# A two-instruction exchange on ScalarE and a reordered close of the last down projection in a one-layer encoder kernel

## The chip, the cores and the metric

The kernel runs as one program on one core of a Trainium2 chip. The metric is the device time of one execution in microseconds, given as the median of several runs. The five engines of the core are called PE (TensorE, matrix products), ACT (ScalarE), DVE (VectorE), POOL (GpSimd) and SP (SyncE, which here only issues DMAs).

## The reference, cut to what matters

One layer of a streaming encoder: two mixers, a cross attention to a memory, and an MLP, each added to the residual stream `h` (512 frames of width 1024), and a final RMSNorm. All is float32. The change lies in the MLP and in the final norm:

```python
def rmsnorm(x, g):
    y = xf * lax.rsqrt(jnp.mean(xf * xf, axis=-1, keepdims=True) + EPS)
    return y * g
...
u = rmsnorm(h, norm_ff_g) @ w1            # (512, 1024) @ (1024, 4096)
h = h + jnp.square(jax.nn.relu(u)) @ w2   # (512, 4096) @ (4096, 1024)
return rmsnorm(h, final_norm_g)           # (512, 1024)
```

## The kernel before

**Precision.** Each float32 operand of a product is split into a high and a low part (`hi` = a rounded copy, made by ACT; `lo` = operand - `hi`, made by DVE at L183, L1549/L1551 or L1580/L1582), and a product is three matmuls: hi x hi, hi x lo, lo x hi.

**The MLP.** The 4096 hidden units are eight groups of 512 (`g` = 0 to 7). Each group's up projection and down projection is a 2 x 2 block product done with seven block products instead of eight, named "1" to "7"; their operands are blocks or sums of blocks (`comb`, `wsum`, `block_sum`). `PRODUCTS` is the order in which PE takes them; the very first group has an order of its own, `FIRST` ("1", "2", "5", "6", "7", "3", "4"). For group 0 the parts of weights and activations are made in an order written out by hand (the `manual_schedule` block at L1798 to L1839); there `split_first("6", "h")` is the ACT copy `whu06` of a summed weight block for product 6, and `x_hi_of("5", slice(0, 2))` is the ACT copy of the first half of the activation sums for product 5 (tile `xs_hi`).

**The last pair.** Groups 0 to 5 are projected down one at a time. Groups 6 and 7 are projected down together at the end (`mlp_down((6, 7))`): for each product in the order 1, 5, 6, 2, 7, 3, 4, PE runs group 6 and then group 7, each for two 128-row halves `t` = 0, 1. A weight block is `wrd` when loaded, `whd` and `wld` when split; the hidden operand's two parts are `hb`. Names carry group and product: `whd63` belongs to group 6, product 3. Products accumulate in PSUM banks `U` (products 1, 6, 7, 4), `Y` (5, 3) and `V` (2), and DVE adds or subtracts a finished bank to `acc` (`add_to`, L1595 and L1597). `acc` has four tiles of 128 frames x 1024: product 3 ends with `acc0` and `acc1`, products 7 and 4 end with `acc2` and `acc3`.

**The close.** `finish` is called when a half row of an `acc` tile is final. For the first half of a tile, ACT takes the sum of squares (`fj`, `fe`), POOL multiplies the half by the norm's weight (`fa`). For the second half of `acc0` and `acc1` it only notes the work in `deferred`. Product 4 is written out in `last_product` (L1659 to L1712) with ACT and DVE in program order: PE takes the rows of `acc2` into bank `U` (to which `onto_rows` had added `acc2`), and those of `acc3` in two column halves, `Z0` and `Z1`. In its shadow ACT and DVE square the rest of `acc0` and `acc1`, POOL raises the sums to the power -1/2 (`fr`, L1720), ACT scales the half with `fa` (`scale_a`, L1728), DVE the other (`scale_b`, L1737), and SP issues the output: tiles 0 and 1 whole (512 KB each), tile 2 in two halves, tile 3 in two halves, one of them from ACT's queue.

**What sets the order.** PE runs in program order throughout. Outside the blocks marked `manual_schedule` a list scheduler orders ACT, DVE, POOL and SP by priority, so moving two instructions can shift others later. Buffers come from rotating pools (four `wh`, four `wl`, twelve of 4 KB per partition tagged `s4`).

Of the kernel before, what the change touches and what calls it, by code (L numbers as in the profile page):

```python
# [13 lines left out]
ALU = mybir.AluOpType  # L14
# [32 lines left out]
def emit(  # L47
# [49 lines left out]
    def s4(shape, name, dt=F32):  # L97
        return s4p.tile([P] + shape, dt, tag="s4", name=name)
# [18 lines left out]
    def mm(name, shape=(S,)):  # L117
        return mmp.tile([P] + list(shape), F32, tag="mm", name=name)
# [10 lines left out]
    def f(a):  # L129
        return a.bitcast(F32)  # L130
# [1433 lines left out]
    hb_order += [(g, name) for name in PRODUCTS for g in (NG - 2, NG - 1)]  # L1564
    hb_used = [0]

    def behind_w4(at, n):
        order_only = mybir.DependencyInfo(mybir.DependencyClass.NoSync, mybir.DependencyReason.DATA)
# [2 lines left out]
    def hidden_part(g, name):  # L1571

        src = comb[g][name]
        hb = s4([2, 2, HS], f"hb{g}{name}", R)
        sign = -1.0 if name == "6" else 1.0
        at = ac.activation(hb[:, 0], src, AF.Copy, scale=sign)
        if g == 0 and name == "1":
            behind_w4(at, 0)
        if name == "6":
            ve.scalar_tensor_tensor(hb[:, 1], src, -1.0, f(hb[:, 0]), op0=ALU.mult, op1=ALU.subtract)  # L1580
        else:
            ve.tensor_tensor(hb[:, 1], src, f(hb[:, 0]), ALU.subtract)  # L1582
        hbs[g, name] = hb

    def hidden_ahead(key, n, within=None):
# [6 lines left out]
    def add_to(ps, rows, half, t, sign):  # L1592
        a = acc[2 * rows + t][:, half * S : (half + 1) * S]
        if sign > 0:
            ve.tensor_tensor(a, ps, a, ALU.add)  # L1595
        else:
            ve.scalar_tensor_tensor(a, ps, -1.0, a, op0=ALU.mult, op1=ALU.add)  # L1597

    PLAN = {
        "1": ("U", True, ()),  # L1600
# [8 lines left out]
    def mlp_down(gs):  # L1609

        end = gs[-1] == NG - 1
        banks = {}
        for n, name in enumerate(PRODUCTS):
            bank, first_, goes = PLAN[name]
            if end and name == PRODUCTS[-1]:
                last_product(gs, banks)
                return
            for g, t in [(g, t) for g in gs for t in range(2)]:
                whi, wlo = unit("d", g, name)
                hidden_ahead((g, name), 1)  # L1620
                hb = hbs[g, name]
                if first_ and g == gs[0]:
                    banks[bank, t] = {"U": sc, "Y": tr}[bank](f"{bank}{g}{t}")
                ps = banks[bank, t]
                ts_ = slice(t * P, (t + 1) * P)
                for k in range(2):
                    hi, lo = hb[:, 0, k, ts_], hb[:, 1, k, ts_]
                    begin = first_ and g == gs[0] and k == 0
                    te.matmul(ps, hi, whi[:, k, :], start=begin, stop=False, skip_group_check=True)  # L1629
                    te.matmul(ps, hi, wlo[:, k, :], start=False, stop=False, skip_group_check=True)  # L1630
                    at = te.matmul(ps, lo, whi[:, k, :], start=False, stop=k == 1, skip_group_check=True)  # L1631
                presum.tick(6 * S / 2400, at)
                if end and (g, t) == (gs[0], 1):
# [12 lines left out]
            hidden_ahead((gs[-1], name), HB, gs)  # L1646
            yield

    onto = []

    def onto_rows(banks):

        u0, u1, a = banks["U", 0], banks["U", 1], acc[3]
        ve.tensor_tensor(u0, u0, acc[2][:, 0:S], ALU.add)
        onto.append(mm("Z1")[:, 0:HS])
        ve.tensor_tensor(onto[0], u1[:, HS:S], a[:, HS:S], ALU.add)
        ve.tensor_tensor(a[:, 0:HS], u1[:, 0:HS], a[:, 0:HS], ALU.add)

    def last_product(gs, banks):  # L1659

        name = PRODUCTS[-1]

        def steps(g, t, cols):
            (whi, wlo), hb = unit("d", g, name), hbs[g, name]
            for k in range(2):
                hi, lo = (hb[:, x, k, t * P : (t + 1) * P] for x in range(2))
                yield from ((hi, whi[:, k, cols]), (hi, wlo[:, k, cols]), (lo, whi[:, k, cols]))

        def product(ps, t, cols, start):
            ops = [op for g in gs for op in steps(g, t, cols)]  # L1670
            for i, (a, b) in enumerate(ops):
                te.matmul(ps, a, b, start=start and i == 0, stop=i == len(ops) - 1, skip_group_check=True)

        with tc.manual_schedule(engines={mybir.EngineType.Activation, mybir.EngineType.DVE}):
            u0 = banks["U", 0]
            product(u0, 0, slice(0, S), False)
            o2, o3 = s4([D], "fo2"), s4([D], "fo3")
            (half, o0, r0_), (_, o1, r1_) = deferred
            hs = slice(half * S, (half + 1) * S)
            e0 = sm(1, "fv0")  # L1680
            ac.activation(o0[:, hs], acc[0][:, hs], AF.Square, scale=1.0 / 32.0, accum_out=e0)
            gp.tensor_tensor(e0, e0, fin[0][0], op=ALU.add)
            row_scale(r0_, e0)
            row_scale(r1_, squares(acc[1][:, hs], o1[:, hs], fin[1][0], "fv1"))
            e2, e3, r2_, r3_ = sm(1, "fv2"), sm(1, "fv3"), sm(1, "fr2"), sm(1, "fr3")
            scale_b(0, half, o0, r0_)
            ac.activation(o2[:, 0:S], u0, AF.Square, scale=1.0 / 32.0, accum_out=e2)
            gp.tensor_tensor(e2, e2, fin[2][0], op=ALU.add)
            row_scale(r2_, e2)
            scale_a(0, o0, r0_)  # L1690
            scale_a(1, o1, r1_)
            scale_b(1, half, o1, r1_)
            for tb, o in ((0, o0), (1, o1)):
                nc.sync.dma_start(out[rows_(tb), :], o)
            h0, h1 = slice(0, HS), slice(HS, S)
            z0, z1 = mm("Z0")[:, 0:HS], onto[0]
            product(z0, 1, h0, True)
            ve.tensor_tensor(acc[3][:, h0], z0, acc[3][:, h0], ALU.add)
            v3 = squares(acc[3][:, h0], o3[:, h0], fin[3][0], "fv30")
            scale_b(2, 0, o2, r2_, u0)  # L1700
            nc.sync.dma_start(out[rows_(2), 0:S], o2[:, 0:S])
            product(z1, 1, h1, False)
            ac.activation(o3[:, h1], z1, AF.Square, scale=1.0 / 32.0, accum_out=e3)
            scale_a(2, o2, r2_)
            dma_a(nc.sync, 2, o2)
            ve.tensor_tensor(e3, e3, v3, ALU.add)
            row_scale(r3_, e3)
            scale_a(3, o3, r3_)
            dma_a(ac, 3, o3)
            for cs, src in ((h0, acc[3][:, h0]), (h1, z1)):  # L1710
                ve.scalar_tensor_tensor(o3[:, cs], src, r3_, gfin[0][:, cs], op0=ALU.mult, op1=ALU.mult)
            nc.sync.dma_start(out[rows_(3), 0:S], o3[:, 0:S])  # L1712

    def squares(a, o, v0, name):
        v = sm(1, name)
# [3 lines left out]
    def row_scale(r, v):  # L1719
        gp.tensor_tensor(r, v, mhalf[:, 0:1], op=ALU.pow)  # L1720
        return r
# [12 lines left out]
    def scale_b(tb, half, o, r, src=None):  # L1734
        cs = slice(half * S, (half + 1) * S)
        src = acc[tb][:, cs] if src is None else src
        ve.scalar_tensor_tensor(o[:, cs], src, r, gfin[half], op0=ALU.mult, op1=ALU.mult)  # L1737


    FINAL = (("2", 0), ("7", 1), ("3", 0))  # L1740
# [2 lines left out]
    def finish(tb, half):  # L1743
# [3 lines left out]
        if tb not in fin:  # L1747
# [4 lines left out]
            gp.tensor_tensor(ag, a[:, cs], gfin[half], op=ALU.mult)  # L1752
# [152 lines left out]
```

## Time and profile before

| what | us |
|---|---|
| median of 3 runs (lowest, highest) | 753.86 (753.45, 754.28) |
| the profiled execution | 753.76 |
| its span, first to last instruction | 751.8 |
| busy in the span: PE | 743.0 (99%) |
| busy in the span: DVE / ACT / POOL | 544.6 / 440.7 / 202.3 |

The span is what the views measure; about 2 us of the execution's own time lie outside it. PE's granted clock was 0.998 of full speed. The last matmul starts at 745.21, so 6.5 us of the span come after it. A timeline row gives start, duration, engine, source line, operation, output <- inputs, shapes and count, and in brackets how long the engine stood idle before it and what ended that. A window row gives for each engine its busy time and instruction count, then PE's clock, the DMA engines' mean busy share and GB/s.

### The profile page before, as it was taken

The page shows a single profiled execution, that of the slowest core. Times are in us where ns is not written, and L with a number is a line of the kernel's source. Part 1 is how long each engine was busy: PE and PEld are TensorE (multiplying, and loading weights), DVE is VectorE, ACT ScalarE, POOL GpSimd, SP SyncE. Part 2 cuts the span into 40 slices and gives each one's busy share as a digit, 9 for nine tenths or more (in the row PEclk, how much of TensorE's full clock was granted, in tenths as well). Part 3 has the DMA queues.
Part 4 walks back from the last instruction along what each step waited for, and adds up shares of the span by engine and source line. Part 5 has one row for each costly group of instructions (what it writes and reads, how often), then busy time and mean ns, then how long its engine had stood idle before and what let it go on. Part 6 is the DMA issues. An engine that isn't in the chain of part 4 may idle for free.

```text
span 751.8 us, 12385 instructions
## 1 busy us (share of the span) xinstructions
PE 743.0 (99%) x4645; PEld 652.7 (87%) x4645; DVE 544.6 (72%) x859; ACT 440.7 (59%) x735; POOL 202.3 (27%) x279
## 2 busy tenths in 40 slices
PE   9999999999999999999999999999999999999996
PEld 6889888888888988888888899898989899999985
DVE  5647873677878756645555799978787887878796
ACT  5655555655666532334434589766566757574863
POOL 7207531233433227621111212111111111100034
PEclk9999999999999999999999999999999999999999
DMA  8641987567957789986578799998989898977452
GB/s 249 200 116 58 307 263 224 182 223 258 294 183 224 261 223 210 196 165 123 121 168 191 118 246 230 245 218 243 239 219 233 221 252 212 243 190 231 134 112 112
DMA packets 109677, 152.92 MB, mean 203 GB/s; under 512 B 6145, under 2 KB 75818, under 8 KB 109618
## 3 DMA queue, kind: packets, MB, share of 16 engines
q1 hardware_dynamic: 85458, 112.52, 45.9%
q0 software_dynamic: 24000, 39.35, 30.3%
q8 instruction: 36, 0.59, 0.3%
q10 hardware_dynamic: 160, 0.27, 0.1%
q14 instruction: 23, 0.19, 0.1%
HBM read 147.91 MB, written 51.40 MB: 265 GB/s over the span
## 4 chain that ended last, share of the span: by engine, by line
PE 91%; DVE 4%; ACT 2%; issue 1%; POOL 1%; DMA 1%; POOLq 0%; SPq 0%; DVEq 0%; ACTq 0%
PE uU L1474 4%; PE uU L1475 4%; PE uU L1473 4%; PE U L1629 3%; PE U L1630 3%; PE U L1631 3%; PE xq L253 2%; PE wo L253 2%; PE xq L254 2%; PE xq L255 2%; PE xw L253 2%; PE xw L254 2%; PE wo L255 2%; PE wo L254 2%; PE uY L1475 2%; PE uY L1474 2%
## 5 line engine op out<-in xcount | busy, mean ns | idle before, releaser
L183 DVE TENSOR_TENSOR wlu<-wru,whu 128x1024 fp32r<-128x1024 f32 x53 | 64.0, 1226 | 26.3 <-ACT whu L179 26.2
L179 ACT ACTIVATE whu<-wru 128x1024 fp32r<-128x1024 f32 x53 | 55.7, 1058 | 41.2 <-PE U L1631 16.8
L183 DVE TENSOR_TENSOR wld<-wrd,whd 128x1024 fp32r<-128x1024 f32 x56 | 69.1, 1236 | 13.8 <-ACT whd L179 13.6
L179 ACT ACTIVATE whd<-wrd 128x1024 fp32r<-128x1024 f32 x56 | 59.0, 1053 | 14.0 <-PE uU L1474 6.3
L1629 PE MATMUL U<-whd,hb 128*128 128x512 f32 x120 | 46.8, 390 | 0.0
L1630 PE MATMUL U<-wld,hb 128*128 128x512 f32 x120 | 46.8, 390 | 0.0
L1631 PE MATMUL U<-whd,hb 128*128 128x512 f32 x120 | 46.7, 389 | 0.0
L1014 POOL TENSOR_SCALAR bi<-nF,Ft 128x128 f32<-128x128 f32 (+3 forms) x32 | 20.8, 656 | 60.4 <-PE pt L1046 33.8
L1474 PE MATMUL uU<-xs_lo,whu 128*128 128x256 f32 x128 | 36.3, 284 | 0.2 <-DVE xs_lo L1549 0.2
L1473 PE MATMUL uU<-xs_hi,whu 128*128 128x256 f32 x128 | 36.3, 284 | 0.0
L1475 PE MATMUL uU<-x_hi,wlu 128*128 128x256 f32 x128 | 36.2, 283 | 0.0
L1473 PE MATMUL uY<-xs_hi,whu 128*128 128x256 f32 x128 | 36.2, 283 | 0.0
L1474 PE MATMUL uY<-xs_lo,whu 128*128 128x256 f32 x128 | 36.2, 283 | 0.0
L1475 PE MATMUL uY<-xs_hi,wlu 128*128 128x256 f32 x128 | 36.2, 283 | 0.0
L1474 PE MATMUL uU<-x_lo,whu 128*128 128x256 f32 x128 | 36.2, 283 | 0.0
L1475 PE MATMUL uU<-xs_hi,wlu 128*128 128x256 f32 x128 | 36.2, 283 | 0.0
L1473 PE MATMUL uU<-x_hi,whu 128*128 128x256 f32 x128 | 36.2, 283 | 0.0
L444 POOL DMA_DIRECT2D wsd<-in_w_dram x16 | 17.8, 1116 | 63.7 <-PE xw L255 12.8
L1369 POOL DMA_DIRECT2D wrd<-in_w_dram x8 | 9.8, 1220 | 86.9 <-DVE wld L183 76.4
L444 POOL DMA_DIRECT2D wsu<-in_w_dram x14 | 17.1, 1220 | 48.2 <-PE xw L255 15.6
L1631 PEld LDWEIGHTS U<-whd,hb 128*128 128x128 f32 x120 | 22.5, 188 | 4.8
L1629 PEld LDWEIGHTS U<-whd,hb 128*128 128x128 f32 x120 | 22.6, 188 | 4.5
(958 smaller groups left out, 2621.2 us busy)
## 6 DMA issues: line engine op xcount, KB each, us to landing
wru<-in_w_dram SPq DMA_DIRECT2D x25, 512.0 KB, 8.0
wsd<-in_w_dram SPq DMA_DIRECT2D x24, 512.0 KB, 7.0
wrd<-in_w_dram SPq DMA_DIRECT2D x24, 512.0 KB, 4.4
wrd<-wsd SPq DMA_DIRECT2D x24, 512.0 KB, 6.0
wsu<-in_w_dram SPq DMA_DIRECT2D x21, 512.0 KB, 6.8
wru<-wsu SPq DMA_DIRECT2D x21, 512.0 KB, 5.8
wsd<-in_w_dram POOLq DMA_DIRECT2D x16, 512.0 KB, 6.6
wsu<-in_w_dram POOLq DMA_DIRECT2D x14, 512.0 KB, 7.1
```

The lines of the kernel that those rows point to most:

```text
L179: at = ac.activation(hi, raw, AF.Copy)
L183: at_lo = ve.tensor_tensor(lo, raw, f(hi), ALU.subtract)
L253: te.matmul(ps, wh, hi, start=n_ == 0 and not begun, stop=False)
L254: te.matmul(ps, wh, lo, start=False, stop=False)
L255: at = te.matmul(ps, wl, hi, start=False, stop=k == order[-1])
L444: yield gp.dma_start(wsum[kind, g, name], src, accum_op=ALU.add, **more)
L1473: te.matmul(ps[:, i, :], whi[:, k, ws], xh[:, k, :], start=begin, stop=False, skip_group_check=True)
L1474: te.matmul(ps[:, i, :], whi[:, k, ws], xl[:, k, :], start=False, stop=False, skip_group_check=True)
L1475: at = te.matmul(ps[:, i, :], wlo[:, k, ws], xh[:, k, :], start=False, stop=k == UK - 1, skip_group_check=True)
L1629: te.matmul(ps, hi, whi[:, k, :], start=begin, stop=False, skip_group_check=True)
L1630: te.matmul(ps, hi, wlo[:, k, :], start=False, stop=False, skip_group_check=True)
L1631: at = te.matmul(ps, lo, whi[:, k, :], start=False, stop=k == 1, skip_group_check=True)
```

## The change

There are three edits. The first exchanges two neighbouring ACT instructions in the hand-written start of the MLP. On ACT, before:

```order
L179 ACTIVATE whu05_4556<-wr05_4504 128x1024
L1538 ACTIVATE xs_hi_4594<-xd5_4562 128x512
L179 ACTIVATE whu06_4601<-wr06_4506 128x1024
L1508 ACTIVATE xg7_4605<-hT3_3287,gv_239 128x512
L1805 ACTIVATE x2_hi_4146<-hT3_3287,gv_239 128x512
L1538 ACTIVATE xs_hi_4594<-xd5_4562 128x512
```

And with the change, on ACT at the same place:

```order
L179 ACTIVATE whu05_4556<-wr05_4504 128x1024
L179 ACTIVATE whu06_4600<-wr06_4506 128x1024
L1539 ACTIVATE xs_hi_4594<-xd5_4562 128x512
L1509 ACTIVATE xg7_4605<-hT3_3287,gv_239 128x512
L1799 ACTIVATE x2_hi_4146<-hT3_3287,gv_239 128x512
L1539 ACTIVATE xs_hi_4594<-xd5_4562 128x512
```

The weight copy for product 6 now stands ahead of the first activation copy for product 5; the rows around them stay. (Line numbers behind the edits differ by a few.) The scheduler also swaps a handful of neighbours in the second group, where the sums of squares of `acc0` and `acc1` (`sj`) now stand ahead of the split of `wru12`.

The second edit changes the order of the last pair's products to 1, 5, 6, 2, 3, 7, 4, takes product 7 by row half first (both groups for `t` = 0, then both for `t` = 1), and does the second half of `finish` for tiles 0 and 1 at once. The third has tile 2 leave as one DMA and tile 3 as one 256 KB half from ACT and two 128 KB quarters from SP. Two order-only dependencies pin DVE: the last low half, `hb74`, ahead of the subtraction that makes `acc2`, and the addition of `acc2` into bank `U` ahead of the two output scalings. On DVE, over the last products, before:

```order
L1582 TENSOR_TENSOR hb73_7776<-s3_7_7562,hb73_7776 128x512
L1582 TENSOR_TENSOR hb64_7779<-sq61_6922,hb64_7779 128x512
L183 TENSOR_TENSOR wld73_7761<-wrd73_7670,whd73_7760 128x1024
L1582 TENSOR_TENSOR hb74_7832<-sq71_7325,hb74_7832 128x512
L183 TENSOR_TENSOR wld64_7783<-wrd66_7465,whd64_7782 128x1024
L1597 SCALAR_TENSOR_TENSOR acc2_4315<-U60_7579,acc2_4315 128x512
L1597 SCALAR_TENSOR_TENSOR acc3_4316<-U61_7586,acc3_4316 128x512
L1654 TENSOR_TENSOR U60_7579<-U60_7579,acc2_4315 128x512
L1656 TENSOR_TENSOR Z1_7813<-U61_7586,acc3_4316 128x256
L1657 TENSOR_TENSOR acc3_4316<-U61_7586,acc3_4316 128x256
L183 TENSOR_TENSOR wld74_7817<-wrd76_7498,whd74_7816 128x1024
L1597 SCALAR_TENSOR_TENSOR acc0_4313<-Y60_7626,acc0_4313 128x512
```

And with the change, on DVE at the same place (`fo0`, `fo1` are the output rows of tiles 0 and 1):

```order
L1585 TENSOR_TENSOR hb64_7779<-sq61_6922,hb64_7779 128x512
L183 TENSOR_TENSOR wld77_7761<-wrd77_7670,whd77_7760 128x1024
L183 TENSOR_TENSOR wld64_7783<-wrd66_7465,whd64_7782 128x1024
L1599 SCALAR_TENSOR_TENSOR acc0_4313<-Y60_7626,acc0_4313 128x512
L1599 SCALAR_TENSOR_TENSOR acc1_4314<-Y61_7633,acc1_4314 128x512
L183 TENSOR_TENSOR wld74_7813<-wrd76_7498,whd74_7812 128x1024
L1585 TENSOR_TENSOR hb74_7828<-sq71_7325,hb74_7828 128x512
L1599 SCALAR_TENSOR_TENSOR acc2_4315<-U60_7579,acc2_4315 128x512
L1648 TENSOR_TENSOR U60_7579<-U60_7579,acc2_4315 128x512
L1728 SCALAR_TENSOR_TENSOR fo0_7793<-acc0_4313,fr0_7794,gfin1_4591 128x512
L1599 SCALAR_TENSOR_TENSOR acc3_4316<-U61_7586,acc3_4316 128x512
L1728 SCALAR_TENSOR_TENSOR fo1_7806<-acc1_4314,fr1_7807,gfin1_4591 128x512
```

The end of `acc0` and `acc1` moves from the last place to the fourth, `hb74` moves behind `wld74`, and the addition into `U` moves behind both. On ACT, likewise, `hb74` now stands behind `whd74` and the squares of `fo0` and `fo1`. On SP the loads `wrd63` and `wrd73` take the places of `wrd67` and `wrd77`, and the other way round.

The diff, cut:

```diff
+    CLOSING = ("1", "5", "6", "2", "3", "7", "4")
...
-        for name in PRODUCTS:
+        for name in CLOSING if gs[-1] == NG - 1 else PRODUCTS:
             for g in gs:
                 add_unit(("d", g, name), [2, S])
...
-            ve.tensor_tensor(hb[:, 1], src, f(hb[:, 0]), ALU.subtract)
+            at_lo[0] = ve.tensor_tensor(hb[:, 1], src, f(hb[:, 0]), ALU.subtract)
...
-            for g, t in [(g, t) for g in gs for t in range(2)]:
+            rows_first = end and name == "7"
+            for g, t in [(g, t) for t in range(2) for g in gs] if rows_first else [(g, t) for g in gs for t in range(2)]:
...
-                    add_to(ps, rows, half, t, sign)
+                    at = add_to(ps, rows, half, t, sign)
+                    if rows_first and t == 0:
+                        tc.add_manual_dep(at.ins, at_lo[0].ins.name, order_only, reason="last low half first")
+                        at_u0.append(ve.tensor_tensor(ps, ps, acc[2][:, 0:S], ALU.add))
...
-            if end and name == "7":
-                onto_rows(banks)
...
+            for tb, (half, o, r_) in enumerate(deferred):
+                scale_a(tb, o, r_)
+                at = scale_b(tb, half, o, r_)
+                tc.add_manual_dep(at.ins, at_u0[0].ins.name, order_only, reason="product 4 first")
+                nc.sync.dma_start(out[rows_(tb), :], o)
+            ve.tensor_tensor(z1, u1[:, h1], a[:, h1], ALU.add)
+            ve.tensor_tensor(a[:, h0], u1[:, h0], a[:, h0], ALU.add)
             product(u0, 0, slice(0, S), False)
...
-            scale_a(0, o0, r0_)
-            scale_a(1, o1, r1_)
-            scale_b(1, half, o1, r1_)
-            for tb, o in ((0, o0), (1, o1)):
-                nc.sync.dma_start(out[rows_(tb), :], o)
+            scale_a(2, o2, r2_)
...
-            nc.sync.dma_start(out[rows_(2), 0:S], o2[:, 0:S])
+            nc.sync.dma_start(out[rows_(2), :], o2)
             product(z1, 1, h1, False)
             ac.activation(o3[:, h1], z1, AF.Square, scale=1.0 / 32.0, accum_out=e3)
-            scale_a(2, o2, r2_)
-            dma_a(nc.sync, 2, o2)
...
                 ve.scalar_tensor_tensor(o3[:, cs], src, r3_, gfin[0][:, cs], op0=ALU.mult, op1=ALU.mult)
-            nc.sync.dma_start(out[rows_(3), 0:S], o3[:, 0:S])
+                nc.sync.dma_start(out[rows_(3), cs], o3[:, cs])
...
-        o, r = s4([D], f"fo{tb}"), sm(1, f"fr{tb}")
+        o, r, e = s4([D], f"fo{tb}"), sm(1, f"fr{tb}"), sm(1, f"fv{tb}")
+        ac.activation(o[:, cs], a[:, cs], AF.Square, scale=1.0 / 32.0, accum_out=e)
+        gp.tensor_tensor(e, e, fin[tb][0], op=ALU.add)
+        row_scale(r, e)
         deferred.append((half, o, r))
...
+        split_first("6", "h")
         x_hi_of("5", slice(0, 2))
-        split_first("6", "h")
```

More of the change, by code (lines that the diff above doesn't have):

```diff
@@ L1563, in emit @@
     hb_order = [(g, name) for g in range(NG - 2) for name in PRODUCTS]
-    hb_order += [(g, name) for name in PRODUCTS for g in (NG - 2, NG - 1)]
+    hb_order += [(g, name) for name in CLOSING for g in (NG - 2, NG - 1)]
     hb_used = [0]
+    at_lo = [None]
     def behind_w4(at, n):
@@ L1594, in add_to @@
         if sign > 0:
-            ve.tensor_tensor(a, ps, a, ALU.add)
-        else:
-            ve.scalar_tensor_tensor(a, ps, -1.0, a, op0=ALU.mult, op1=ALU.add)
+            return ve.tensor_tensor(a, ps, a, ALU.add)
+        return ve.scalar_tensor_tensor(a, ps, -1.0, a, op0=ALU.mult, op1=ALU.add)
     PLAN = {
@@ L1612, in mlp_down @@
         banks = {}
-        for n, name in enumerate(PRODUCTS):
+        for name in CLOSING if end else PRODUCTS:
             bank, first_, goes = PLAN[name]
-            if end and name == PRODUCTS[-1]:
+            if end and name == CLOSING[-1]:
                 last_product(gs, banks)
                 return
-            for g, t in [(g, t) for g in gs for t in range(2)]:
+            rows_first = end and name == "7"
+            for g, t in [(g, t) for t in range(2) for g in gs] if rows_first else [(g, t) for g in gs for t in range(2)]:
                 whi, wlo = unit("d", g, name)
@@ L1632, in mlp_down @@
                 presum.tick(6 * S / 2400, at)
-                if end and (g, t) == (gs[0], 1):
+                if end and (g, t) == ((gs[1], 0) if rows_first else (gs[0], 1)):
                     hidden_ahead((g, name), HB + 1)
@@ L1674, in last_product @@
         with tc.manual_schedule(engines={mybir.EngineType.Activation, mybir.EngineType.DVE}):
-            u0 = banks["U", 0]
-            product(u0, 0, slice(0, S), False)
[L1677 to L1686, printed above, removed]
+            u0, u1, a = banks["U", 0], banks["U", 1], acc[3]
+            o2, o3 = s4([D], "fo2"), s4([D], "fo3")
+            e2, e3, r2_, r3_ = sm(1, "fv2"), sm(1, "fv3"), sm(1, "fr2"), sm(1, "fr3")
+            h0, h1 = slice(0, HS), slice(HS, S)
+            z0, z1 = mm("Z0")[:, 0:HS], mm("Z1")[:, 0:HS]
+            for tb, (half, o, r_) in enumerate(deferred):
+                scale_a(tb, o, r_)
+                at = scale_b(tb, half, o, r_)
+                order_only = mybir.DependencyInfo(mybir.DependencyClass.NoSync, mybir.DependencyReason.DATA)
+                tc.add_manual_dep(at.ins, at_u0[0].ins.name, order_only, reason="product 4 first")
+                nc.sync.dma_start(out[rows_(tb), :], o)
+            ve.tensor_tensor(z1, u1[:, h1], a[:, h1], ALU.add)
+            ve.tensor_tensor(a[:, h0], u1[:, h0], a[:, h0], ALU.add)
+            product(u0, 0, slice(0, S), False)
             ac.activation(o2[:, 0:S], u0, AF.Square, scale=1.0 / 32.0, accum_out=e2)
@@ L1689, in last_product @@
             row_scale(r2_, e2)
[L1690 to L1696 removed]
+            scale_a(2, o2, r2_)
             product(z0, 1, h0, True)
[L1698 to L1699 removed]
+            ve.tensor_tensor(a[:, h0], z0, a[:, h0], ALU.add)
+            v3 = squares(a[:, h0], o3[:, h0], fin[3][0], "fv30")
             scale_b(2, 0, o2, r2_, u0)
[L1701 removed]
+            nc.sync.dma_start(out[rows_(2), :], o2)
             product(z1, 1, h1, False)
             ac.activation(o3[:, h1], z1, AF.Square, scale=1.0 / 32.0, accum_out=e3)
[L1704 to L1705 removed]
             ve.tensor_tensor(e3, e3, v3, ALU.add)
@@ L1709, in last_product @@
             dma_a(ac, 3, o3)
-            for cs, src in ((h0, acc[3][:, h0]), (h1, z1)):
+            for cs, src in ((h0, a[:, h0]), (h1, z1)):
                 ve.scalar_tensor_tensor(o3[:, cs], src, r3_, gfin[0][:, cs], op0=ALU.mult, op1=ALU.mult)
-            nc.sync.dma_start(out[rows_(3), 0:S], o3[:, 0:S])
+                nc.sync.dma_start(out[rows_(3), cs], o3[:, cs])
     def squares(a, o, v0, name):
@@ L1736, in scale_b @@
         src = acc[tb][:, cs] if src is None else src
-        ve.scalar_tensor_tensor(o[:, cs], src, r, gfin[half], op0=ALU.mult, op1=ALU.mult)
+        return ve.scalar_tensor_tensor(o[:, cs], src, r, gfin[half], op0=ALU.mult, op1=ALU.mult)
     FINAL = (("2", 0), ("7", 1), ("3", 0))
```

11 lines of the change are left out of this document (3 added, 8 removed).

## The prediction

> **What bounds the kernel now.** I read the chain of waits first, for the engine that sets the time. This is its share line on the page:
>
> ```profile
> PE 91%; DVE 4%; ACT 2%; issue 1%; POOL 1%; DMA 1%; POOLq 0%; SPq 0%; DVEq 0%; ACTq 0%
> ```
>
> PE carries the span, and the change takes no matmul away. So only two things can move the time: a place where PE waits, and the stretch behind its last matmul. The waits of PE name one place in the MLP. PE's timeline there, then those of ACT and DVE:
>
> ```profile
> 438.65 0.28 PE L1473 MATMUL uU<-xs_hi,whu 128*128 128x256 f32 x1
> 439.17 0.39 PE L1474 MATMUL uU<-xs_lo,whu 128*128 128x256 f32 x1 [0.24 <-DVE xs_lo L1549]
> 439.51 0.29 PE L1473 MATMUL uU<-xs_hi,whu 128*128 128x256 f32 x1
> 439.63 0.28 PE L1474 MATMUL uU<-xs_lo,whu 128*128 128x256 f32 x1
> ...
> 429.99 0.63 ACT L1538 ACTIVATE xs_hi<-xd 128x512 fp32r<-128x512 f32 x1 [1.50 <-PE xw L254]
> 430.53 1.05 ACT L179 ACTIVATE whu<-wr 128x1024 fp32r<-128x1024 f32 x1
> 436.79 1.06 ACT L1538 ACTIVATE xs_hi<-xd 128x1024 fp32r<-128x1024 f32 x1 [0.24 <-DVE xd L1523]
> ...
> 431.61 1.23 DVE L183 TENSOR_TENSOR wlu<-wr,whu 128x1024 fp32r<-128x1024 f32 x1 [0.70 <-ACT whu L179]
> 437.89 1.23 DVE L1549 SCALAR_TENSOR_TENSOR xs_lo<-xd,xs_hi 128x1024 fp32r<-128x1024 f32 x1 [0.53 <-ACT xs_hi L1538]
> ```
>
> A matmul of this size starts 0.12 after the one before (439.51 to 439.63). The three from 438.65 to 439.51 should take 0.36 and take 0.86: PE loses **0.50** to the low half of product 6, `xs_lo`, which ends at 439.12.
>
> For the tail, the chain from the last matmul to the last output, and the output issues:
>
> ```profile
> 745.21 0.28 PE L1672 MATMUL Z<-whd,hb 128*128 128x256 f32 x1
> 746.09 0.16 DVE L1706 TENSOR_TENSOR fv<-fv,fv 128x1 f32<-128x1 f32 x1 [0.23 <-ACT fo L1703]
> 746.33 0.54 POOL L1720 TENSOR_TENSOR fr<-fv,mhalf 128x1 f32<-128x1 f32 x1 [1.60 <-DVE fv L1706]
> 746.91 0.48 DVE L1711 SCALAR_TENSOR_TENSOR fo<-acc,fr,gfin 128x256 f32<-128x256 f32 x1 [0.66 <-POOL fr L1720]
> 747.31 0.48 DVE L1711 SCALAR_TENSOR_TENSOR fo<-Z,fr,gfin 128x256 f32<-128x256 f32 x1
> ...
> 743.98 0.97 SPq L1694 DMA_DIRECT2D out_dram<-fo  x2
> 745.89 0.33 SPq L1701 DMA_DIRECT2D out_dram<-fo  x1
> 747.66 0.42 ACTq L1732 DMA_DIRECT2D out_dram<-fo  x1
> 747.81 0.33 SPq L1712 DMA_DIRECT2D out_dram<-fo  x1
> ```
>
> The DMA traffic from 742 to 752 in 40 slices of 0.25, and the window over its busy part:
>
> ```profile
> GB/s 0 0 0 0 0 0 0 0 0 0 0 279 442 360 442 426 377 410 393 393 393 344 393 401 369 377 401 385 377 377 385 352 311 33 0 0 0 0 0 0
> 744.75:750.25 5.50, 0.73 (x7) 0.53 (x5) 2.15 (x6) 1.81 (x4) 0.54 (x1) 0.81 0.98 381
> ```
>
> This is the finding: all 2.1 MB of output leave in one unbroken run at 381 GB/s with the DMA engines 0.98 busy, from about 0.85 after the first issue to about 750.3. The last issue at 747.81 stands behind tiles 0, 1 and 2. The span ends at 751.8, 1.5 after the data. Tiles 0 and 1 start so late because product 3 ends them late:
>
> ```profile
> 740.00 1.28 DVE L1597 SCALAR_TENSOR_TENSOR acc<-Y,acc 128x512 f32<-128x512 f32 x2
> 740.72 0.63 ACT L1681 ACTIVATE fo<-acc 128x512 f32<-128x512 f32 x1 [2.98 <-DVE acc L1597]
> 742.92 1.42 DVE L1737 SCALAR_TENSOR_TENSOR fo<-acc,fr,gfin 128x512 f32<-128x512 f32 x2 [0.73 <-POOL fr L1720]
> ```
>
> **The exchange on ACT.** Both instructions wait for the same matmul, so `whu06` now starts at 429.99, 0.54 earlier. DVE stood idle for it (0.70), so `wlu06` starts 0.54 earlier, and so does all behind it: DVE and ACT then wait for each other (0.24 and 0.53 in the rows). The copy put second ends by 431.7 (1.05 and 0.63 after 429.99); its first reader on DVE stands behind `wlu06` and three others. `xs_lo` then ends at 438.58, before PE wants it at 438.77. Gain **0.50**, with 0.13 to spare after a signal of about 0.05; the bounds are 0 and 0.50. The ripples in the second group change no row on which PE waits now, and I price them at nothing.
>
> **Product 3 ahead of 7.** PE's work is the same, 24 matmuls from 734.29 to 739.73 in either order. What must be checked is what PE now needs sooner. The rows of the last products, from DVE, ACT, POOL, PE and SP:
>
> ```profile
> 729.77 1.42 DVE L1582 TENSOR_TENSOR hb<-s,hb 128x512 fp32r<-128x512 f32 x1
> 731.11 1.78 DVE L1582 TENSOR_TENSOR hb<-sq,hb 128x512 fp32r<-128x512 f32 x1
> 732.82 1.21 DVE L183 TENSOR_TENSOR wld<-wrd,whd 128x1024 fp32r<-128x1024 f32 x1
> 733.95 0.68 DVE L1582 TENSOR_TENSOR hb<-sq,hb 128x512 fp32r<-128x512 f32 x1
> 734.56 1.21 DVE L183 TENSOR_TENSOR wld<-wrd,whd 128x1024 fp32r<-128x1024 f32 x1
> 735.69 1.28 DVE L1597 SCALAR_TENSOR_TENSOR acc<-U,acc 128x512 f32<-128x512 f32 x2
> 736.89 0.68 DVE L1654 TENSOR_TENSOR U<-U,acc 128x512 f32<-128x512 f32 x1
> ...
> 734.49 1.07 ACT L179 ACTIVATE whd<-wrd 128x1024 fp32r<-128x1024 f32 x1 [1.52 <-PE U L1631]
> 736.40 0.63 ACT L1749 ACTIVATE fj<-acc 128x512 f32<-128x512 f32 x1 [0.84 <-DVE acc L1597]
> ...
> 729.34 3.00 POOL L1752 TENSOR_TENSOR fa<-acc,gfin 128x512 f32<-128x512 f32 x2 [10.80 <-DVE acc L1595]
> 742.30 1.11 POOL L1720 TENSOR_TENSOR fr<-fv,mhalf 128x1 f32<-128x1 f32 x2
> 743.42 0.30 POOL L1688 TENSOR_TENSOR fv<-fv,fe 128x1 f32<-128x1 f32 x1
> ...
> 734.29 0.39 PE L1629 MATMUL Y<-whd,hb 128*128 128x512 f32 x1
> 739.73 0.39 PE L1672 MATMUL U<-whd,hb 128*128 128x512 f32 x1
> ...
> 707.04 11.31 SPq L1351 DMA_DIRECT2D wrd<-in_w_dram  x3
> ```
>
> *Weights.* `wld77` takes `wld73`'s slot (732.82 to 734.03). Product 7 by row halves wants it 6 matmuls (1.36) after 734.29 instead of 12, so it has 1.6 to spare. The loads of products 3 and 7 trade places in one SP queue, whose last load is issued by 718.4; nothing but outputs is queued behind. Price 0.
>
> *The pinned addition into `U`.* PE's first matmul of product 4, at 739.73, needs it, and it used to end at 737.57. Now: `wld64` follows `wld77` without `hb74` between, 733.95 to 735.16. The two endings of `acc0` and `acc1` take 1.28, 735.08 to 736.36. `wld74` takes 736.28 to 737.49 (`whd74` is there at 735.56). On ACT the two squares start at 735.8 and 736.4 (0.63 apart), and `hb74`'s high half ends near 737.65. Its low half takes 737.69 to 738.37, `acc2` follows 0.60 behind each start, 738.29, and the addition runs 738.89 to **739.57**: 0.16 ahead of PE, or 0.1 after the signal. I take a price of 0; the bounds are 0 and 0.4.
>
> What could eat that is POOL. The two `hb` rows of 1.42 and 1.78 fall under POOL's two 128x512 products (729.34 to 732.34); the one of 0.68 does not. So a DVE instruction with both inputs in SBUF waits out such a product. During `hb74` POOL has only `fv` and `fr` of one column. The row at 742.30 says they do not hold DVE up: the two `fr` run until 743.41, and the scalings begun at 742.92 still take 1.42 for two, as undisturbed.
>
> The Trainium skill (SBUF — State Buffer, Who interferes with whom) says otherwise for any size: whichever of the two engines starts first gets the shared port for its whole instruction, and the other blocks. By that rule one `fr` of 0.55 ahead of `hb74` would add about 0.4 to the sum.
>
> *Scalings ahead of `Z1`.* POOL's `fa2` starts behind `acc2`, near 739.1, and lasts up to 1.5. The output scaling of tile 0 waits it out and ends near 741.1, that of tile 1, behind `acc3`, near 742.4; `Z1` is then ready near 742.8, or some 743.5 if POOL's next product, `fa3`, gets partly in front. PE wants it 24 matmuls after 739.73 (12 of 0.227, 12 of 0.12), at 743.9. Price 0. On ACT `scale_a(2)` now stands ahead of the square of the last `Z`; it waits for `fr2`, which comes behind `fa3` on POOL, and I price that at 0 to 0.1.
>
> **The outputs.** Tiles 0 and 1, scaled by 741.1 and 742.4, flow from 742 and are out by about 744.7 (2 x 1.38). Tile 2, whole, waits for the scaling of its second half, which ends at 745.86 now; with PE 0.50 earlier it is issued at 745.36, flows from 746.2, and at 381 GB/s (1.38 for 512 KB) is out by 747.6. Tile 3's first quarter is issued when its scaling ends, 747.39 - 0.50 = 746.89, and flows from 747.75, into an empty queue; the half from ACT follows at 747.16 + 0.85 = 748.0, the last quarter at 748.16. From 747.75 the queue has 512 KB: 1.38, to 749.13. That is 1.2 before 750.3: 0.50 from the exchange and **0.7** from the queue.
>
> **The sum.** 0.50 + 0.7 = 1.2 off the profiled 753.76, or 752.55. The median of the runs is 0.1 above the profiled execution, so **752.6**.
>
> **Rivals.**
>
> *The landing does not shorten.* For the outputs the view of DMA issues gives:
>
> ```profile
> out_dram<-fo SPq DMA_DIRECT2D x3, 256.0 KB, 3.0
> ```
>
> If the last issue lands 3.0 later whatever the queue holds, only the exchange counts: 753.86 - 0.50 = 753.35. Against it: the engines are 0.98 busy until the data end. Chance 0.13. The Trainium skill (DMA: Bandwidth & Descriptors, Anatomy of one DMA) gives such a rule, about 2.0 us fixed plus bytes at 436 GB/s; by it 128 KB instead of 256 KB would land 0.3 sooner, 753.05.
>
> *The pieces flow as if alone.* The half from ACT, 256 KB from 748.0 at 381 GB/s, ends at 748.7, with the quarters beside it: 1.65 off, 752.2, or 752.0 with a shorter end. For it: slices of 442 occur. Chance 0.18.
>
> *The pinned chain overruns.* If `fr0`, `fv1` and `fr1` (0.55 + 0.3 + 0.55 = 1.4) all pass ahead of `hb74`, the addition ends at 740.97, PE waits 1.3, and all behind moves: 753.9, slightly slower than before. It decides from an addition ending after 739.66, and gives all back from 740.9. Against it: the row at 742.30. Chance 0.10, mostly for a part of it (753.0).
>
> *The exchange brings nothing,* if 0.13 is not enough at 438.77: 753.1. Chance 0.05.
>
> **How the numbers follow.** My forecast has 0.54, its own range 752.2 to 752.9. A measurement of this kernel tells about 0.2%, 1.5 us, from no change: faster means below 752.35, slower above 755.4. Faster takes most of the second rival and the lower edge of the forecast, 0.25; slower only what I do not see, 0.03; the same 0.72. The range takes in the rivals up to half of the overrun: 751.9 to 753.5.
>
> **What would show it.** PE's starts 438.65 to 439.51 at 0.12 each, with everything behind 0.50 earlier. No wait of PE on the addition into `U`. Output traffic with gaps, tiles 0 and 1 out before 745, and an end of data near 749.1. A PE wait at product 4's start, or one unbroken run of DMA up to the end, would prove me wrong.

## The result and the profile after

The changed kernel takes 752.54 us (median of 20 runs, 752.15 to 753.12), the kernel before 754.05 (753.39 to 754.42) on the same chip: the ratio is 0.9981, 95% interval 0.9975 to 0.9987. The profiled execution takes 752.49 instead of 753.76, its span is 750.7 instead of 751.8.

**The exchange.** PE's timeline at the start of product 6, as in the rows of before at 438.65:

```profile
438.55 0.28 PE L1476 MATMUL uY<-xs_hi,wlu 128*128 128x256 f32 x1
438.67 0.28 PE L1474 MATMUL uU<-xs_hi,whu 128*128 128x256 f32 x1
438.79 0.28 PE L1475 MATMUL uU<-xs_lo,whu 128*128 128x256 f32 x1
438.91 0.28 PE L1476 MATMUL uU<-xs_hi,wlu 128*128 128x256 f32 x1
```

All steps are 0.12; the wait for `xs_lo` is gone. The low half itself now runs 437.37 to 438.60.

**The last pair.** Timeline rows of DVE, PE and POOL in the changed kernel:

```profile
735.80 1.21 DVE L183 TENSOR_TENSOR wld<-wrd,whd 128x1024 fp32r<-128x1024 f32 x1
737.21 0.69 DVE L1585 TENSOR_TENSOR hb<-sq,hb 128x512 fp32r<-128x512 f32 x1 [0.20 <-ACT hb L1579]
738.42 0.69 DVE L1648 TENSOR_TENSOR U<-U,acc 128x512 f32<-128x512 f32 x1
739.01 1.41 DVE L1728 SCALAR_TENSOR_TENSOR fo<-acc,fr,gfin 128x512 f32<-128x512 f32 x1
...
739.03 0.39 PE L1634 MATMUL U<-whd,hb 128*128 128x512 f32 x1
739.25 0.47 PE L1669 MATMUL U<-whd,hb 128*128 128x512 f32 x1
739.56 0.40 PE L1669 MATMUL U<-wld,hb 128*128 128x512 f32 x1
...
736.18 0.88 POOL L1748 TENSOR_TENSOR fv<-fv,fe 128x1 f32<-128x1 f32 x1 [2.59 <-ACT fo L1747]
737.14 0.58 POOL L1711 TENSOR_TENSOR fr<-fv,mhalf 128x1 f32<-128x1 f32 x1
738.58 1.29 POOL L1743 TENSOR_TENSOR fa<-acc,gfin 128x512 f32<-128x512 f32 x1
```

The addition into `U` ends at 739.11, as forecast (739.57 less the 0.50). PE's first matmul of product 4 starts on its beat at 739.25, and no wait is written beside it. But it lasts 0.47 instead of 0.39, and the next starts 0.31 later instead of 0.23: PE loses a little here that it did not lose before.

**The close.** The last matmul, POOL's last `fr`, the output issues; then the DMA traffic from 742 to 752 in slices of 0.25, the windows over the three stretches of output traffic, and the last row of the DMA issues:

```profile
744.85 0.28 PE L1669 MATMUL Z<-whd,hb 128*128 128x256 f32 x1
745.98 0.54 POOL L1711 TENSOR_TENSOR fr<-fv,mhalf 128x1 f32<-128x1 f32 x1 [2.04 <-DVE fv L1697]
740.50 1.60 SPq L1682 DMA_DIRECT2D out_dram<-fo  x2
745.54 0.33 SPq L1694 DMA_DIRECT2D out_dram<-fo  x1
747.07 0.81 SPq L1703 DMA_DIRECT2D out_dram<-fo  x2
747.30 0.38 ACTq L1723 DMA_DIRECT2D out_dram<-fo  x1
```

```profile
GB/s 377 410 377 426 393 426 393 246 0 33 0 0 0 0 0 0 0 246 393 410 426 442 180 90 360 393 377 369 336 172 0 0 0 0 0 0 0 0 0 0
```

```profile
741.33:744.05 2.72, 2.72 (x22) 2.56 (x21) 1.34 (x4) 1.22 (x5) 2.38 (x4) 1.00 0.95 386
746.37:747.80 1.43, 0.00 (x0) 0.00 (x0) 0.88 (x2) 0.72 (x1) 0.15 (x1) 1.00 0.90 367
747.90:749.48 1.58, 0.00 (x0) 0.00 (x0) 0.00 (x0) 0.00 (x0) 0.00 (x0) 0.77 0.90 331
```

```profile
out_dram<-fo SPq DMA_DIRECT2D x2, 128.0 KB, 2.3
```

The one unbroken run of output has become three: tiles 0 and 1 (out by 744.05), tile 2, and tile 3 by itself from 747.90 to 749.48. The last output data end at 749.48 instead of 750.37.

**Where the time went.** Since single executions differ (below), I compare the same matmuls in each trace. The table gives how much later than in the profile of before the same matmul starts: at 30, at the first matmul of product 6 (438.65 in before), behind product 6's first rows (440.5), and at the last matmul of all. The last columns are lengths, from the start of the last matmul to the end of the output data and to the end of the span.

| kernel (profiled execution) | at 30 | product 6 | behind it | last matmul | to data end | to span end | median, runs |
|---|---|---|---|---|---|---|---|
| before | 0 | 0 | 0 | 0 | 5.16 | 6.55 | 754.05, 20 |
| changed | -0.02 | 0.01 | -0.48 | -0.35 | 4.63 | 5.89 | 752.54, 20 |
| e1 exchange alone | 0.70 | 0.70 | 0.21 | 0.22 | 5.19 | 6.57 | 753.33, 11 |
| e2 no exchange | 0.57 | 0.57 | 0.57 | 0.69 | 4.63 | 5.90 | 753.15, 11 |
| e3 old pieces | 0.44 | 0.44 | -0.05 | 0.05 | 4.88 | 6.14 | 752.85, 11 |
| e4 addition first | 0.57 | 0.59 | 0.10 | 0.11 | 4.63 | 5.90 | 752.56, 11 |
| e5 before, tiles 0 and 1 not sent | -0.28 | -0.27 | -0.27 | -0.26 | 4.88 | 6.28 | 753.66, 11 |
| e6 changed, tile 2 not sent | 0.47 | 0.46 | -0.03 | 0.11 | 4.63 | 5.96 | 752.73, 11 |
| e7 low half unpinned | 0.62 | 0.62 | 0.12 | 0.14 | 4.63 | 5.89 | 752.45, 11 |
| e8 addition first again | 0.11 | 0.11 | -0.39 | -0.37 | 4.63 | 5.91 | 752.41, 11 |
| e9 changed again | 0.62 | 0.63 | 0.13 | 0.23 | 4.64 | 5.90 | 752.76, 11 |
| e10 tile 3's half whole | 0.19 | 0.23 | -0.27 | -0.15 | 4.88 | 6.21 | 752.88, 8 |

From before to changed: -0.48 at product 6, +0.13 from there to the last matmul, -0.65 behind it, together -1.0, which is the difference of the two spans. The medians of the runs differ by 1.5 here (by the interval 1.0 to 1.9), and by 1.1 in the second batch (e9, 752.76, beside 753.85 for before).

The medians show more than the traces because part of the difference lies outside the span. In the kernel before, an execution takes 2.0 us longer than its span (1.96 to 2.08 in the runs beside the experiments), in the changed kernel 1.76 (1.70 to 1.82 in its two batches). So the profiled execution is 1.27 faster: 1.01 in the span and 0.26 outside it. By the spans alone, the medians of e9's batch differ by 0.8, those of e8's by 1.1, where the marks of the table give 1.05 and 1.12. The same 0.2 to 0.3 outside the span are gone in e1 (1.72 on average), which has only the exchange, and in e2 (1.80), which has all but the exchange, and are still there in e5 (2.02). No run tells what they are.

### The profile page after: what moved, and what is told of

Same layout as the page of the kernel before. It is cut to its first block, busy times and chain, and to the rows that moved or that the text cites. A ratio compares the mean times of both kernels' runs of the same rounds, so it can differ in the third digit from the quotient of the medians.

```text
span 750.7 us, 12389 instructions
## 1 busy us (share of the span) xinstructions
PE 742.9 (99%) x4645; PEld 653.1 (87%) x4645; DVE 543.7 (72%) x857; ACT 441.8 (59%) x737; POOL 203.1 (27%) x280
## 4 chain that ended last, share of the span: by engine, by line
PE 94%; ACT 1%; DVE 1%; issue 1%; POOL 1%; DMA 1%; POOLq 0%; SPq 0%; DVEq 0%; ACTq 0%
PE uU L1474 4%; PE uU L1476 4%; PE uU L1475 4%; PE U L1632 4%; PE U L1633 4%; PE U L1634 4%; PE uY L1475 2%; PE uY L1476 2%; PE uY L1474 2%; PE xq L253 2%; PE wo L253 2%; PE xq L254 2%; PE xw L253 2%; PE xq L255 2%; PE wo L254 2%; PE xw L254 2%
```

## The experiments

**e1: the exchange alone,** on the kernel before:

```diff
-        x_hi_of("5", slice(0, 2))
         split_first("6", "h")
+        x_hi_of("5", slice(0, 2))
```

> The kernel before with the first edit alone: the high half of block 6 goes ahead of the first half copy of product 5 on ScalarE. Theory: PE stops losing 0.50 at the low half of product 6, and nothing behind gives it back, so the last matmul starts at 744.71 instead of 745.21, every output issue is 0.5 earlier, the one unbroken run of output stays 5.5 long, and the time is 754.05 - 0.50 = 753.55. Rival 1, the exchange brings nothing because something else holds the low half: 754.05, PE's wait still there. Rival 2, the 0.13 us that the changed kernel loses in product 4 comes with the exchange (work around product 4 then meets it at another time): last matmul at 744.85, 753.7.

Its PE timeline (this execution stands 0.70 behind that of before from the start on, so product 6 begins at 439.35):

```profile
439.23 0.28 PE L1475 MATMUL uY<-xs_hi,wlu 128*128 128x256 f32 x1
439.35 0.28 PE L1473 MATMUL uU<-xs_hi,whu 128*128 128x256 f32 x1
439.47 0.28 PE L1474 MATMUL uU<-xs_lo,whu 128*128 128x256 f32 x1
439.59 0.28 PE L1475 MATMUL uU<-xs_hi,wlu 128*128 128x256 f32 x1
...
745.42 0.28 PE L1672 MATMUL Z<-whd,hb 128*128 128x256 f32 x1
```

No wait, 0.49 gained (0.70 to 0.21), and nothing of it is lost up to the last matmul (0.22). The median is 753.33 beside 753.89 for before, ratio 0.9994 (0.9985 to 1.0003); 0.30 of these 0.56 lie outside the span, so the 0.49 rest on the trace and not on the median. So the exchange does what it says, and product 4's loss is not its doing.

**e2: the changed kernel without the exchange** (the same two lines, the other way).

> The changed kernel with the two high halves on ScalarE put back in their old order; the product order, the early outputs and the three pieces stay. Theory: the edits add, so it is 0.50 slower than the changed kernel, 752.54 + 0.50 = 753.04, or 1.0 faster than before by the outputs alone; PE loses its 0.50 at product 6 again. The 0.13 of product 4 stays, because the addition into U and PE move together. Rival, the last landing comes a fixed time after the last issue: then the outputs are worth nothing and it is 754.05. Rival 2, the queue was what the exchange had to pass: then the exchange is worth nothing here and it stays at 752.54.

PE's timeline there, and at product 4:

```profile
439.22 0.28 PE L1474 MATMUL uU<-xs_hi,whu 128*128 128x256 f32 x1
439.74 0.39 PE L1475 MATMUL uU<-xs_lo,whu 128*128 128x256 f32 x1 [0.23 <-DVE xs_lo L1550]
...
740.32 0.47 PE L1669 MATMUL U<-whd,hb 128*128 128x512 f32 x1
740.63 0.39 PE L1669 MATMUL U<-wld,hb 128*128 128x512 f32 x1
```

The wait is back, product 4 loses its 0.12 as in the changed kernel, the close is as short (5.90). The median is 753.15 (before 753.89; 0.9989, 0.9979 to 0.9998). The edits add; the rival of a fixed landing is out.

**e3: the outputs cut as before,** with everything else changed:

```diff
-            scale_a(2, o2, r2_)
...
-            nc.sync.dma_start(out[rows_(2), :], o2)
+            nc.sync.dma_start(out[rows_(2), 0:S], o2[:, 0:S])
...
+            scale_a(2, o2, r2_)
+            dma_a(nc.sync, 2, o2)
...
-                nc.sync.dma_start(out[rows_(3), cs], o3[:, cs])
+            nc.sync.dma_start(out[rows_(3), 0:S], o3[:, 0:S])
```

> The changed kernel with the outputs of the last two tiles cut as before: tile 2 in two halves, the second behind the last square on ScalarE, and tile 3's half of SyncE in one piece behind both scalings. Theory (what is queued ahead counts): tiles 0 and 1 are out of the way as in the changed kernel, so most of the 0.7 stays. The last issue comes at about 747.45 instead of 747.55 but with 256 KB, and the second half of tile 2 is issued at about 746.35; the last 768 KB then end near 749.5 instead of 749.3, so 752.7, 0.2 over the changed kernel. Rival, the gain comes from the small last pieces (a landing that grows with the bytes of one issue): then nearly all of it goes, 753.3 to 753.5. Rival 2, the pieces do nothing: 752.5.

The row of its DMA issues (median from issue to landing last):

```profile
out_dram<-fo SPq DMA_DIRECT2D x3, 256.0 KB, 2.6
```

A landing takes 2.6 instead of 3.0 with the same bytes. The close is 6.14, 0.25 longer than in the changed kernel (752.85 beside 753.89; 0.9984, 0.9976 to 0.9993). Tiles 0 and 1 out of the way bring the larger part of the close, the pieces 0.25. Which piece, e10 tells.

**e4: the addition into `U` ahead of the low half:**

```diff
-                if end and (g, t) == ((gs[1], 0) if rows_first else (gs[0], 1)):
+                if end and not rows_first and (g, t) == (gs[0], 1):
                     hidden_ahead((g, name), HB + 1)
...
-                        tc.add_manual_dep(at.ins, at_lo[0].ins.name, order_only, reason="last low half first")
                         at_u0.append(ve.tensor_tensor(ps, ps, acc[2][:, 0:S], ALU.add))
+                        hidden_ahead((g, name), HB + 1)
+                        tc.add_manual_dep(at_lo[0].ins, at_u0[0].ins.name, order_only, reason="addition first")
```

> The changed kernel with the addition of block 2 into U put ahead of the last low half on VectorE (the order is pinned the other way round). It tests where product 4 loses 0.13 (2.85 from its first matmul to the next product, 2.72 before). Theory A, the addition ends too near PE's first matmul (739.11 against 739.25), and PE needs its signal some 0.2 sooner than the start: now the addition ends near 738.3, product 4 takes 2.72 again, the last matmul starts at 744.71, and the time is 752.54 - 0.14 = 752.4. Theory B, PE is slowed by what VectorE and ScalarE do in PSUM while product 4 begins, not by the wait: product 4 still takes 2.85, 752.5. Rival that speaks against it: the low half now falls under GpSimd's product of block 2, ends past 741.1, and PE waits for it: 752.6 or more.

Timeline rows of DVE and PE:

```profile
738.13 0.68 DVE L1646 TENSOR_TENSOR U<-U,acc 128x512 f32<-128x512 f32 x1
738.72 0.67 DVE L1585 TENSOR_TENSOR hb<-sq,hb 128x512 fp32r<-128x512 f32 x1
...
739.84 0.39 PE L1670 MATMUL U<-whd,hb 128*128 128x512 f32 x1
740.07 0.39 PE L1670 MATMUL U<-wld,hb 128*128 128x512 f32 x1
```

The addition ends 1.03 ahead of PE, the first matmul takes 0.39, the next comes 0.23 later, and from product 6 to the last matmul PE loses 0.01 instead of 0.13. Theory A holds. Against theory B speaks the changed kernel itself: behind the addition, which ends at 739.11, neither DVE nor ACT touches PSUM before 740.35, and the slow step is over by 739.56. The median does not show it (752.56); neither the one nor the other batch tells 0.13.

**e7: the low half unpinned** (the line with "last low half first" left out).

> The changed kernel without the dependency that puts the last low half on VectorE ahead of block 2's ending; the scheduler then writes: ending of block 2, low half, addition into U. Both halves of the question are in it: how near the rival of the overrun was, and what lead PE wants. In the times of the changed kernel, the ending of block 2 can start when the weight copy is done, 737.0, so the low half starts near 737.6 and the addition near 738.2, ending 738.9, 0.2 ahead of where it ends now. If PE's loss of 0.13 comes from a lead of 0.14, a lead of 0.35 should cost 0 to 0.05: 752.4. If GpSimd gets its product of block 2 in ahead of the low half, the low half takes 1.4 instead of 0.7, the addition ends at 739.6 and PE loses 0.5 or more: 753.0.

DVE, POOL and PE there:

```profile
738.15 0.68 DVE L1585 TENSOR_TENSOR hb<-sq,hb 128x512 fp32r<-128x512 f32 x1
738.75 0.69 DVE L1646 TENSOR_TENSOR U<-U,acc 128x512 f32<-128x512 f32 x1
...
737.75 0.58 POOL L1709 TENSOR_TENSOR fr<-fv,mhalf 128x1 f32<-128x1 f32 x1
738.32 0.56 POOL L1746 TENSOR_TENSOR fv<-fv,fe 128x1 f32<-128x1 f32 x1
739.48 1.76 POOL L1741 TENSOR_TENSOR fa<-acc,gfin 128x512 f32<-128x512 f32 x1
...
739.87 0.39 PE L1667 MATMUL U<-whd,hb 128*128 128x512 f32 x1
740.10 0.39 PE L1667 MATMUL U<-wld,hb 128*128 128x512 f32 x1
```

The addition ends 0.43 ahead of PE and costs nothing. POOL comes to its large product only at 739.48, behind `fr` and `fv`, so even without the pin the low half is not held up. The median is 752.45.

**e5: the kernel before without the outputs of tiles 0 and 1:**

```diff
-            for tb, o in ((0, o0), (1, o1)):
-                nc.sync.dma_start(out[rows_(tb), :], o)
```

> The kernel before with the two output transfers of tiles 0 and 1 left out (those 256 rows of the output are not written; all arithmetic stays). It takes 1 MB out of the queue ahead of the last pieces and moves nothing else. Theory (what is queued ahead counts): the last two issues stay at 747.66 and 747.81 (from the same span start), but find an emptier queue; the second half of tile 2, issued at 746.69, flows from 747.5 to 748.2, the 512 KB of tile 3 from 748.5 to about 749.9 instead of 750.3, or a little more where packets of the last piece start late: the stretch from the last matmul to the end of the span shrinks by 0.4, as in the kernel with early outputs and old pieces. Rival, the last landing comes a fixed 3.0 after the last issue whatever the queue holds: the stretch stays as it is. Rival 2, all of the 0.65 comes from the queue and the pieces only matter by chance: the stretch shrinks by 0.65.

DMA traffic from 748 to 752 in slices of 0.1 (its last matmul starts at 744.95):

```profile
GB/s 62 0 0 266 430 389 348 369 369 451 389 369 348 369 369 451 266 62 82 0 0 0 0 0 0 0 0 0 0 0 0 0 0 0 0 0 0 0 0 0
```

The queue now has gaps, and the data end 4.88 after the last matmul instead of 5.16: 0.28, less than the 0.4 expected. The 512 KB of tile 3 alone run from 748.3 to 749.83, about 1.5. The median is 753.66 beside 754.06 (0.9995, 0.9986 to 1.0004).

**e10: only tile 3's half of SyncE in one piece,** tile 2 whole:

```diff
-                nc.sync.dma_start(out[rows_(3), cs], o3[:, cs])
+            nc.sync.dma_start(out[rows_(3), 0:S], o3[:, 0:S])
```

> The changed kernel with only SyncE's half of tile 3 in one piece behind both scalings again; tile 2 still leaves whole. It tells which of the pieces carries the 0.25 that the kernel with all the old pieces lost. Theory: the first quarter of tile 3 starts the flow of its 512 KB 0.3 earlier; without it the flow starts with ScalarE's half, and the stretch from the last matmul to the end of the span goes from 5.89 back to 6.14, as with all the old pieces. Rival, it was tile 2's cut in two: the stretch stays at 5.89, or 5.95 at most.

The same slices (its last matmul starts at 745.06):

```profile
GB/s 0 0 0 0 205 471 348 389 348 389 369 471 369 348 349 369 389 348 82 0 0 0 0 0 0 0 0 0 0 0 0 0 0 0 0 0 0 0 0 0
```

Tile 3 begins to flow at 748.42, 3.36 after the last matmul, in the changed kernel 3.05 after it (747.90 less 744.85); the data end 4.88 after it, as in e3. So the 0.25 is the first quarter of tile 3, which starts the flow 0.31 earlier, and for the end of the data it does not matter whether tile 2 leaves whole or in halves. The span ends 6.21 after the last matmul, 0.07 later than in e3 and than expected; that part lies behind the data. The median is 752.88 beside 753.81 (0.9987, 0.9976 to 0.9998).

**e6: the changed kernel without the output of tile 2** (its one `dma_start` left out).

> The changed kernel with the output transfer of tile 2 left out (128 rows of the output are not written; all arithmetic stays). Theory: in the changed kernel tile 2's data end just before tile 3's begin, so tile 3 already flows as if alone, at the rate of one 512 KB transfer in three pieces: nothing changes, 0 to 0.1 off, 752.5. Rival, tile 2 still holds tile 3 up (the two run into each other): 0.3 or more off, 752.2.

DMA traffic from 742 to 752, slices of 0.25:

```profile
GB/s 377 410 393 410 377 442 442 393 426 148 33 0 0 0 0 0 0 0 0 0 0 0 0 0 0 147 381 397 393 324 344 111 0 0 0 0 0 0 0 0
```

The data end 4.63 after the last matmul, as with tile 2; the span ends 5.96 after it instead of 5.89, and the median is 752.73. In the changed kernel tile 3 already flows as if alone.

**e8 and e9: the kernel of e4 and the changed kernel once more,** on one chip.

> The kernel with the addition into U put first once more, on one chip with the changed kernel. By the traces it is 0.13 faster in product 4; executions of one kernel spread over some 0.9, so the medians of 11 runs should differ by 0.1 and hardly tell it: 0.0 to 0.3 under the changed kernel.

> The changed kernel once more, beside the kernel with the addition into U put first. The same trace from the first 15 us on: product 4 loses 0.13, the stretch from the last matmul to the end of the span is 5.9. If the spread between executions comes from the start of the kernel alone, its marks stand off from the earlier trace by one constant behind 15 us. Time about 752.5.

The medians are 752.41 and 752.76. e8 loses 0.02 between product 6 and the last matmul, e9 0.10. The addition put first is thus better by about 0.1 in every trace, and the runs alone (their intervals against before are 0.9971 to 0.9989 and 0.9975 to 0.9993) do not tell the two apart. How executions of one kernel differ is told at the end.

## Why the prediction was right, and where its steps were off

The forecast was 752.6 with 1.2 off the profiled execution; 752.54 was measured, and the traces account for 1.0.

*The exchange* was to bring 0.50: 0.48 in the changed kernel, 0.49 in e1, and `xs_lo` ended at 438.60 where 438.58 was forecast. The 0.13 to spare was enough.

*Product 3 ahead of 7* was to cost nothing. The path that I worked out came true: the addition ends at 739.11 (forecast, less 0.50, 739.07), `wld77` holds nobody up, `Z1` is ready at 742.03 (forecast 742.3), `scale_a(2)` ends 0.5 ahead of the last square. The step that failed is "0.1 after the signal, price 0": I took any lead as enough. All six traces with a lead of 0.14 to 0.15 (changed, e2, e3, e6, e9, e10) lose 0.08 to 0.09 at this one step; 0.43 (e7) and 1.03 (e4) lose nothing there. The changed kernel's 0.13 holds another 0.05 that creeps in over the next ten matmuls; e2, e6 and e10 have 0.02 to 0.04 of it, e3 and e9 none, and its cause stays open. The bounds of 0 and 0.4 held it.

*What POOL does to the low half* was read rightly from the row at 742.30: `fr` runs from 737.14 to 737.72 beside `hb74`, which takes 0.69, and in e7 0.68. The large product does what it did before: `fo` at 739.01 takes 1.41 under `fa`. The Trainium skill (SBUF — State Buffer, Who interferes with whom) would have had the first of the two block the other. The trace agrees for the large product, and the other way round (`fv` at 736.18 takes 0.88 while `wld` runs, 0.19 at 743.13 with DVE idle), but not for an `fr` of one column ahead of DVE.

*The outputs* were to bring 0.7: they brought 0.65, but not as worked out. I gave all of it to the queue and let tile 3 flow at 381 GB/s for 1.38. It starts 0.15 later than forecast, at 747.90, and takes 1.58 at 331, so the data end at 749.48 and not at 749.13: 0.9 earlier than before where the sum had 1.2. Three terms stand in its place: 0.28 from tiles 0 and 1 out of the queue (e5), 0.25 from the first quarter of tile 3 (e10), and 0.12 because the span ends 1.26 after the data instead of 1.38. The last term I had not seen. In before, e1 and e5 a DMA of 8 KB of instructions comes at the very end (the 82 in the last slice of e5), in the changed kernel around 744.5 (the 33 in its slices). But e6 and e10 have it early as well and end 1.33 after the data, so its cause stays open.

*The rivals.* A landing 3.0 after the last issue is refuted: the quarters land 2.3 after theirs. In e3, with tiles 0 and 1 gone, 256 KB land 2.6 after their issue, where they landed 3.0 after it behind a full queue. The rule of the Trainium skill (DMA: Bandwidth & Descriptors, Anatomy of one DMA) gives, as an estimate, 2.0 + 0.3 for 128 KB and 2.0 + 0.6 for 256 KB, though it is fitted there on GpSimd's path; the 2.3 and 2.6 agree, and the 3.0 of before is 0.4 above it. The second rival, in which ACT's half ends by 748.7 with the quarters beside it, is out too: nothing else holds tile 3 up (e6), and still its pieces together flow at 331 GB/s, below the 381 of the full queue. The chain did not overrun, though 0.13 of that rival's kind came. That the exchange brings nothing is out by e1.

*Where the agreement is partly luck.* The sum of my terms was 1.2. The profiled executions differ by 1.27, but only 1.01 of it lies in the span; the 0.26 outside the span was in no term, and it makes up for what the sum had too much. The 0.65 beside my 0.7 for the outputs is luck in the same way: the data account for 0.53, and the 0.12 of the earlier end of the span was not forecast.

## What to carry to other kernels

An engine that is listed without a wait can still lose time to a result that comes only just ahead of it: compare the step between two instructions with the same step elsewhere, and give a pinned chain more lead than it seems to need (0.14 us cost something here, 0.43 nothing). When a run of output fills the DMA queue to the end, early tiles help only until the last tile flows alone; from there the time is set by when its first piece is issued, so a small first piece helps (128 KB here). Effects below the spread of the runs are read between the same two instructions of each trace, not from the end of the span or from medians, which also hold what lies outside the span.

## What the runs showed that I had not expected

**The spread between the traces comes from the first 15 us.** Timeline rows of PE from the changed kernel, and from the same kernel run again:

```profile
4.73 0.66 PE L499 MATMUL xn<-ident,xt 128*128 128x128 f32 x4
5.23 1.03 PE L534 MATMUL warm<-zero 128*128 128x512 bf16 x4
6.43 0.70 PE L545 MATMUL gf<-hn_hi,wh0a 128*128 128x512 f32 x2 [0.18 <-DVE wh0a L181]
29.93 0.39 PE L253 MATMUL gf<-hn_hi,wh1a 128*128 128x512 f32 x1
```

```profile
4.74 1.12 PE L499 MATMUL xn<-ident,xt 128*128 128x128 f32 x4
5.65 1.79 PE L534 MATMUL warm<-zero 128*128 128x512 bf16 x4
7.00 0.91 PE L545 MATMUL gf<-hn_hi,wh0a 128*128 128x512 f32 x2
30.57 0.39 PE L253 MATMUL gf<-hn_hi,wh1a 128*128 128x512 f32 x1
```

The first transposes take 1.12 instead of 0.66, the first matmuls on them come 0.6 later, and from 15 us on the kernel keeps this distance: 0.64 in these rows at 30, 0.62 at product 6, 0.58 at the last matmul. The two profiled executions took 752.49 and 753.11, which is 0.62 apart. Over all twelve traces this start lies between -0.28 and 0.70, while the stretch from 30 to product 6 is the same to 0.04. What holds PE up is its clock: in the trace's record of the granted clock full speed begins at 4.66 here and at 7.19 in the second run, and the `warm` matmuls (fillers that keep PE busy) follow each other at 0.21 in the one and at 0.43 in the other. In eight traces full speed comes between 6.17 (e8) and 7.29 (e1), and the later it comes, the later PE is at 7 us, 0.28 in e8 and 0.84 in e1, by half of the difference. In the other four (before, changed, e5, e7) it comes between 4.07 and 4.66; e7 is late all the same, because there PE waits 1.08 for DVE's `wh0a` at 7.17. Why the clock rises at different times was not tried.

**A matmul whose input is almost late holds up the next, with no wait listed.** With its input 0.14 to 0.15 ahead, the first matmul of product 4 is listed with 0.47 instead of 0.39 and the next starts 0.08 to 0.09 late, in six traces out of six; with 0.43 or more, in three out of three, neither is seen.

**The rate of an output goes with its pieces.** In the changed kernel it is 386 GB/s for tiles 0 and 1 together, 367 for tile 2 whole and 331 for tile 3 in three pieces, the last two with the DMA engines busy 0.90 of the time. In e10 tile 3 leaves in two halves and takes 1.52, which is 345. The pieces are issued one after the other, and part of this may be the wait for the next piece; that was not tried.
